# Seven block products in place of eight in the FFN up projections, with the down projection as a phase of its own

## The chip, the core and the metric

The kernel runs on one core of one Trainium2 chip. The metric is the device time of one execution in microseconds (us). Its engines, as the profile names them: PE (TensorE, matrix multiply), PEld (its weight loads, which run beside PE), DVE (VectorE), ACT (ScalarE), POOL (GpSimd), and SP, which only issues DMAs here. Each engine takes its instructions strictly in the order in which they were written into its queue, and waits on semaphores.

## What is computed

A decoder trunk of two layers on x of 1024 tokens by 1024 channels, in float32. Layer 0 has an attention mixer, layer 1 a gated recurrent one (RG-LRU); each is followed by a gated FFN with a short causal convolution, and a last norm ends the trunk. The change touches the two FFNs and what hands x to them:

```python
def conv_ffn(h, w_up, conv_w, conv_b, w_down):        # h 1024x1024, w_up 1024 x 5632
    u = causal_dwconv(h @ w_up, conv_w, conv_b)       # 3 taps along the tokens
    return (jax.nn.silu(u[..., :D_FF]) * u[..., D_FF:]) @ w_down   # D_FF 2816

x = x + mix                                           # for each layer
x = x + conv_ffn(rmsnorm(x, norm_ffn[layer]), f_w_up[layer], ...)
```

## The kernel before

Channels lie on the 128 partitions and tokens along a row, so x is 8 channel chunks (KC) by two token halves of 512 (HT). Every matmul multiplies a 128x128 weight block by a 128x512 operand in fp32r. To keep the precision, an operand is split into a rounded `hi` (ACT, L107 or L123) and the rest `lo` (DVE, L108 or L124), and `mm3` (L116) issues three matmuls: hi by hi, hi by lo, lo by hi (L118 to L120).

The FFN (`ffn`, L275) works through 22 chunks of 128 of the 2816 hidden channels. A chunk needs two up units, its gate half and its value half. `units` (L135) makes one unit with 2 halves x 8 KC x 3 = 48 matmuls into one of four PSUM tiles `U`. Its operand `H` (tiles hh and hl) is x times the norm's gain, made chunk by chunk in `norm_add` (L166) as each piece of x gets its last addend; the norm's factor per token, `R`, is multiplied in after the matmuls, when DVE takes the unit out of PSUM (L291). `rstd` (L198) makes R meanwhile from sums of squares: ACT squares each piece (L183), POOL adds the squares up (L187), PE sums over the partitions with a matrix of ones (L202), ACT takes Ln and Exp (L195, L196). After R comes the convolution (`conv`, L214: one ACT pass, then two DVE passes, L219 and L221), silu (ACT, L294), the product (DVE, L295) and the split into yh and yl, which stay in SBUF.

The down projection runs between the up units: after each group of four chunks (`UP_GROUPS`, L46) `down` (L231) multiplies the group's y by its weights, again with `mm3`, and DVE adds the result to x in SBUF (L227). The last group goes through `down_last` (L246), which hands each finished piece of x to the next norm. Weights come by SP from DRAM, 512 KB a transfer (L95), into two raw buffers `wr`, and are split into wh and wl.

The order on each engine is not the order of the code: a scheduler of the programming layer, which weighs priorities and free buffers, lays the instructions of all engines into their queues when the program is built. Every wait for a buffer that it hands out is part of that order.

Of the kernel before, what the change touches and what calls it, by code (L numbers as in the profile page):

```python
# [48 lines left out]
def half_of(h):  # L49
    return slice(h * HT, h * HT + HT)  # L50


class Kern:
# [62 lines left out]
    def mm3(self, out, whi, wlo, xhi, xlo, first, last):  # L116
        mm = self.nc.tensor.matmul
        mm(out, whi, xhi, start=first, stop=False)  # L118
        mm(out, whi, xlo, start=False, stop=False)  # L119
        mm(out, wlo, xhi, start=False, stop=last)  # L120
# [110 lines left out]
    def down(self, wsrc, ng, ys, bias=None):  # L231
        nf = 8 // ng
        for ft in range(8 // nf):
            w = self.load_w(wsrc(ft))
            for fi in range(nf):
                f = ft * nf + fi
                U = self.newU("D")
                for half in range(2):
                    sl = half_of(half)
                    for k in range(ng):  # L240
                        ws = slice((fi * ng + k) * P, (fi * ng + k + 1) * P)
                        self.mm3(U[:, sl], w[0][:, ws], w[1][:, ws], ys[k][0][:, sl], ys[k][1][:, sl], k == 0, k == ng - 1)
                for half in range(2):
                    self.accum(f, half, U[:, half_of(half)], bias)

    def down_last(self, wsrc, ng, ys, fin):  # L246
# [3 lines left out]
        for sl in fin.slices:  # L250
# [4 lines left out]
            for f0 in range(0, 8, 2):  # L255
                U = self.newU("D")
                for i in range(2):
                    f = f0 + i
                    w = ws_[f // nf]
                    for k in range(ng):  # L260
                        s = slice(((f % nf) * ng + k) * P, ((f % nf) * ng + k + 1) * P)
                        self.mm3(U[:, i * HT:i * HT + n], w[0][:, s], w[1][:, s], ys[k][0][:, sl], ys[k][1][:, sl], k == 0, k == ng - 1)
# [11 lines left out]

    def ffn(self, l, nm, fin):  # L275
        nc, io = self.nc, self.io
        fw, fb = f"fw{l}", f"fb{l}"
        with ExitStack() as st:
            hp = st.enter_context(self.pool(f"ffh{l}"))
            tp = st.enter_context(self.pool(f"fft{l}"))  # L280
            srcs = [io["wup"][l, ci, k] for ci in range(NFF) for k in range(2)]
            gen = self.units(srcs, nm["H"], 3, lambda: self.rstd(nm))
            ups = {}
            tmp = lambda: tp.tile([P, S], FP, tag="c", bufs=5, name=self.nm("c"))

            def up(ci):
                t = []
                for k in range(2):
                    U = next(gen)
                    z, o = tmp(), tmp()  # L290
                    nc.vector.tensor_tensor(z, U, nm["R"], op=OP.mult)  # L291
                    self.conv(o, z, (fw, fb), k * NFF + ci, 3)
                    t.append(o)
                nc.scalar.activation(t[0], t[0], AF.Silu)  # L294
                nc.vector.tensor_tensor(t[0], t[0], t[1], op=OP.mult)  # L295
                hi = hp.tile([P, S], FR, tag="y", bufs=10, name=self.nm("yh"))
                lo = hp.tile([P, S], FR, tag="y", bufs=10, name=self.nm("yl"))
                ups[ci] = self.split(hi, lo, t[0])

            def dn(g):  # L300
                c0, n = UP_GROUPS[g]
                ys = [ups.pop(c0 + i) for i in range(n)]
                if g == len(UP_GROUPS) - 1:
                    self.down_last(lambda ft: io["wdl"][l, ft], n, ys, fin)
                else:
                    self.down(lambda ft: io["wd"][l, g, ft], n, ys)

            for g, (c0, n) in enumerate(UP_GROUPS):
                last = g == len(UP_GROUPS) - 1
                for i in range(n):  # L310
                    up(c0 + i)
                    if i == (n - 1 if last else 0) and g > 0:
                        dn(g - 1)
            dn(len(UP_GROUPS) - 1)
# [25 lines left out]
    def rglru(self, nm, fin):  # L340
        nc, io = self.nc, self.io
        with ExitStack() as st:
            hp = st.enter_context(self.pool("rgh"))
            tp = st.enter_context(self.pool("rgt"))
            self.W2 = st.enter_context(self.pool("rgw"))
# [73 lines left out]
            G(7), Y(7), O(2), O(3)  # L419
            self.W2 = None  # L420

# [456 lines left out]
    def even_layer(self, fin):  # L878
# [4 lines left out]
        self.yd = [dp.tile([P, S], FP, name=f"yd{k}") for k in range(KC)]  # L883

# [253 lines left out]

class FinalNorm:
# [56 lines left out]
def open_main(k):  # L1196
# [3 lines left out]
    xp = k.ctx.enter_context(k.pool("X"))  # L1200
    k.X = [[xp.tile([P, HT], FP, name=f"x{c}_{h}") for h in range(2)] for c in range(KC)]
    k.np = k.ctx.enter_context(k.pool("np"))
    k.Rp = k.ctx.enter_context(k.pool("Rp"))
    hp = k.ctx.enter_context(k.pool("H"))
    k.Hp = [hp, hp]
    k.hbufs = 32

# [4 lines left out]
def trunk(tc, io, stages):  # L1212
    with ExitStack() as ctx:
# [5 lines left out]
        def finisher(i):  # L1219
            return NextNorm(k, GI[seq[i + 1]]) if i + 1 < len(seq) else FinalNorm(k)  # L1220
# [7 lines left out]
        else:  # L1228
            open_main(k)
            nm = k.new_norm(GI[seq[0]])  # L1230
            for half in range(2):
                for c in range(KC):
                    nc.sync.dma_start(k.X[c][half], io["x"][c, :, half_of(half)])
                    k.norm_add(nm, c, half, k.X[c][half])
# [30 lines left out]
```

## Time and profile before

| what | value |
|---|---|
| median of 3 runs | 2441.83 us (2440.38 to 2443.75) |
| the profiled execution | 2435.48 us, of which the span from first to last instruction is 2433.6 us |
| granted TensorE clock, mean over the span | 0.987 of full |
| attention layer's mixer | 0 to about 655 us |
| FFN of layer 0 | about 655 to 1388 us |
| recurrent mixer of layer 1 | about 1388 to 1690 us |
| FFN of layer 1, last norm, output | about 1690 to 2434 us |

A row of a group is read as: line, engine, operation, out<-in by the program's names, shapes, xcount, then the time in which the group was busy, the mean of one instruction, the engine's idle time before them and what ended it. In a timeline, a bracket behind a row gives the idle time of the engine before it and what it waited for. A matmul's own duration (about 0.39 us) covers its way through the array, and the next one starts before it ends, so the pace is the distance of two starts.

### The profile page before, as it was taken

What the parts mean: (1) busy time and instruction counts of PE and PEld (TensorE: products, weight loads), DVE (VectorE), ACT (ScalarE), POOL (GpSimd) and SP (SyncE); (2) the same over time, 40 slices, a digit from 0 to 9 for tenths busy, and PEclk for the clock granted to TensorE, in tenths of its full rate; (3) what the DMA queues carried; (4) which work ended last, traced back from release to release, by engine and by line L of the source; (5) the groups of instructions that cost most, each with busy time, mean ns of one, the idle gap of its engine ahead of it and who ended that gap; (6) DMA issues with size and microseconds to landing.
All of it is one profiled execution on the core that took longest, in us unless ns stands there. A gap on an engine that the chain in (4) does not pass through costs nothing.

```text
span 2433.6 us, 26552 instructions
## 1 busy us (share of the span) xinstructions
PE 2347.1 (96%) x10690; PEld 1925.2 (79%) x10690; DVE 1468.8 (60%) x2008; ACT 993.8 (41%) x1391; POOL 213.1 (9%) x151
## 2 busy tenths in 40 slices
PE   7899899999999999999999999999999999999997
PEld 5788777777688888888888777887888888888886
DVE  6456878988855453545455766768554535354556
ACT  5652767766632131213132465584322213131224
POOL 3002223211300000000000300003000000000001
PEclk9899999999999999999999999999999999999998
DMA  4113112222411111111111111111111111111111
GB/s 141 57 54 117 53 53 79 87 78 86 152 45 52 44 52 44 52 53 44 52 44 52 46 39 65 48 38 35 52 44 52 48 48 52 44 52 46 50 52 70
DMA packets 49435, 144.35 MB, mean 59 GB/s; under 512 B 5536, under 2 KB 9120, under 8 KB 49184
## 3 DMA queue, kind: packets, MB, share of 16 engines
q1 hardware_dynamic: 47808, 139.25, 16.7%
q8 instruction: 83, 1.36, 0.2%
q0 software_dynamic: 640, 2.10, 0.2%
q10 hardware_dynamic: 864, 1.32, 0.2%
q14 instruction: 40, 0.33, 0.0%
HBM read 130.06 MB, written 12.58 MB: 59 GB/s over the span
## 4 chain that ended last, share of the span: by engine, by line
PE 74%; DVE 8%; ACT 3%; issue 3%; POOL 1%; DMA 0%; DVEq 0%; SPq 0%; POOLq 0%; ACTq 0%
PE U L120 15%; PE U L119 15%; PE U L118 15%; PE D L118 7%; PE D L119 7%; PE D L120 7%; DVE hl L172 2%; PE T L764 2%; PE O L747 2%; PE F L118 1%; PE F L119 1%; PE F L120 1%; DVE P L739 1%; DVE x L266 1%; DVE P L722 1%
## 5 line engine op out<-in xcount | busy, mean ns | idle before, releaser
L118 PE MATMUL U<-hh,wh 128*128 128x512 f32 x1888 | 741.8, 393 | 16.6 <-ACT wh L107 15.0
L120 PE MATMUL U<-hh,wl 128*128 128x512 f32 x1888 | 741.8, 393 | 7.2 <-DVE wl L108 7.2
L119 PE MATMUL U<-hl,wh 128*128 128x512 f32 x1888 | 740.9, 393 | 7.6 <-DVE hl L172 7.6
L107 ACT ACTIVATE wh<-wr 128x1024 fp32r<-128x1024 f32 x208 | 220.5, 1060 | 833.4 <-PE U L119 469.5
L118 PEld LDWEIGHTS U<-hh,wh 128*128 128x128 f32 x1888 | 357.2, 189 | 94.6 <-ACT wh L107 16.6
L120 PEld LDWEIGHTS U<-hh,wl 128*128 128x128 f32 x1888 | 356.9, 189 | 87.5 <-DVE wl L108 12.2
L119 PEld LDWEIGHTS U<-hl,wh 128*128 128x128 f32 x1888 | 357.4, 189 | 85.6 <-DVE hl L172 10.3
L291 DVE TENSOR_TENSOR c<-U,R 128x1024 f32<-128x1024 f32 x88 | 107.8, 1225 | 388.5 <-PE U L120 371.4
L118 PE MATMUL D<-yh,wh 128*128 128x512 f32 (+1 forms) x720 | 278.0, 386 | 0.0
L119 PE MATMUL D<-yl,wh 128*128 128x512 f32 (+1 forms) x720 | 277.2, 385 | 0.0
L120 PE MATMUL D<-yh,wl 128*128 128x512 f32 (+1 forms) x720 | 277.2, 385 | 0.0
L227 DVE TENSOR_TENSOR x<-D,x 128x512 f32<-128x512 f32 x192 | 123.6, 685 | 236.7 <-PE D L120 236.6
L108 DVE TENSOR_TENSOR wl<-wr,wh 128x1024 fp32r<-128x1024 f32 x184 | 231.7, 1260 | 48.6 <-ACT wh L107 45.4
L221 DVE SCALAR_TENSOR_TENSOR c<-c,par,c 128x1023 f32<-128x1023 f32 (+1 forms) x176 | 225.7, 1283 | 17.9 <-ACT c L219 15.0
L187 POOL TENSOR_TENSOR sq<-sq,sq 128x512 f32<-128x512 f32 x56 | 89.1, 1597 | 1036.4 <-ACT sq L183 995.7
L118 PEld LDWEIGHTS D<-yh,wh 128*128 128x128 f32 x720 | 135.8, 189 | 27.2 <-DVE x L266 0.2
L119 PEld LDWEIGHTS D<-yl,wh 128*128 128x128 f32 x720 | 135.8, 189 | 27.1 <-issue 0.2
L120 PEld LDWEIGHTS D<-yh,wl 128*128 128x128 f32 x720 | 135.8, 189 | 26.7
L219 ACT ACTIVATE c<-c,par 128x1024 f32<-128x1024 f32 x88 | 109.6, 1245 | 37.4 <-DVE c L291 37.4
L123 ACT ACTIVATE yh<-c 128x1024 fp32r<-128x1024 f32 x44 | 46.7, 1060 | 175.4 <-DVE c L295 159.8
L724 ACT ACTIVATE P<-P,m 128x640 f32<-128x640 f32 (+7 forms) x128 | 93.5, 730 | 46.4 <-DVE m L722 46.0
L124 DVE TENSOR_TENSOR pl<-T,ph 128x512 fp32r<-128x512 f32 x132 | 89.3, 686 | 28.7 <-ACT ph L123 26.1
(258 smaller groups left out, 2938.4 us busy)
## 6 DMA issues: line engine op xcount, KB each, us to landing
wr<-in_wup SPq DMA_DIRECT2D x88, 512.0 KB, 3.2
wr<-in_wd SPq DMA_DIRECT2D x40, 512.0 KB, 3.2
wr<-in_wbc SPq DMA_DIRECT2D x24, 512.0 KB, 3.4
wr<-in_cin SPq DMA_DIRECT2D x16, 512.0 KB, 3.2
yd<-y SPq DMA_DIRECT2D x24, 256.0 KB, 2.3
x<-in_x SPq DMA_DIRECT2D x16, 256.0 KB, 5.8
wr<-in_wob SPq DMA_DIRECT2D x8, 512.0 KB, 3.3
y<-in_x SPq DMA_DIRECT2D x16, 256.0 KB, 2.6
```

The costliest lines, as they stand in the source:

```text
L107: nc.scalar.activation(hi[:, s], raw[:, s], AF.Copy)
L108: eng.tensor_tensor(lo[:, s], raw[:, s], hi[:, s].bitcast(FP), op=OP.subtract)
L118: mm(out, whi, xhi, start=first, stop=False)
L119: mm(out, whi, xlo, start=False, stop=False)
L120: mm(out, wlo, xhi, start=False, stop=last)
L124: (eng or self.nc.vector).tensor_tensor(lo, t, hi.bitcast(FP), op=OP.subtract)
L187: eng.tensor_tensor(acc, acc, t, op=OP.add)
L219: nc.scalar.activation(o, src, AF.Identity, bias=b, scale=w(K - 1))
L221: nc.vector.scalar_tensor_tensor(o[:, s:], src[:, :n - s], w(K - 1 - s), o[:, s:], op0=OP.mult, op1=OP.add)
L227: nc.vector.tensor_tensor(x, ps, x, op=OP.add)
L291: nc.vector.tensor_tensor(z, U, nm["R"], op=OP.mult)
L724: nc.scalar.activation(p, p, AF.Exp, bias=m, scale=-1.0, accum_out=s)
```

## The change

Of a hidden chunk, the gate and value halves of the weights (128 channels each) by the two halves of the input channels (512 each) make a 2x2 block matrix a11, a12, a21, a22; the normed x, by the two halves of the input channels and the two halves of the tokens, makes b11, b12, b21, b22. The plain product takes eight block products. The changed `ffn` takes seven (`up_units`), each of 4 KC x 3 = 12 matmuls of 128x512, from sums of blocks.

- Sums of weight blocks, per chunk: four POOL adds of 128x512 (`up_sums`, into tiles z: s1 and s2 in one, s3 and s4 in the other), then splits of z on ACT and DVE (tiles sh and sl; ah and al for a22). Two buffers of each.
- Sums of x blocks, once per layer: 16 POOL adds (`ProductNorm.finish`), and splits into "pages": 56 tiles hi and lo for the seven operands.
- R and the gain are now multiplied into x before it is split (`ProductNorm.half`, 16 DVE operations of 128x512 per layer), so the operand exists only once R does. The operation after PSUM (L291 before) goes.
- The seven products accumulate in three PSUM banks A, Bk, C of a chunk. `begin(i + 1)` (products "1" and "2") is written ahead of `rest(i)` (products "6", "5", "7", "3", "4"); ACT copies of 128x512 (L337, L348, L350, L356 in the new numbering) and three DVE adds take the four results out.
- x itself is stored to DRAM (xd) before the FFN and loaded back after the up phase, and its SBUF serves the up phase. The gated values go to DRAM through POOL's queue (fd), 512 KB each, and come back for the down phase, which runs after all 22 chunks; their split into hi and lo moves there.
- The recurrent mixer closes its temporary pools before its last `down`.

The core of the diff:

```diff
+    def up_sums(self, raws):
+        p = self.nc.gpsimd
+        a11, a12, a21, a22 = (raws[k][:, half_of(h)] for k in range(2) for h in range(2))
...
+        p.tensor_tensor(s1, a21, a22, op=OP.add)
+        p.tensor_tensor(s2, s1, a11, op=OP.subtract)
+        p.tensor_tensor(s3, a11, a21, op=OP.subtract)
+        p.tensor_tensor(s4, a12, s2, op=OP.subtract)
...
+        w12 = self.split(t(S, "sh", 2), t(S, "sl", 2), sa)
+        w34 = self.split(t(S, "sh", 2), t(S, "sl", 2), sb)
+        wa = self.split(t(HT, "ah", 2), t(HT, "al", 2), a22)
...
+        def begin(i):
+            raws[i] = self.up_raw(srcs[i])
+            w = self.split_w(raws[i][0])
...
+            self.product(A, at(0), B["1"], True)
+            nc.scalar.activation(z[0][:, :HT], A, AF.Copy)
+            self.product(C, at(1), B["2"], True)
+            nc.vector.tensor_tensor(z[0][:, :HT], C, z[0][:, :HT], op=OP.add)
...
+        def rest(i):
...
+            self.product(A, w["6"], B["6"], False)
+            nc.scalar.activation(c12, A, AF.Copy)
+            self.product(Bk, w["5"], B["5"], True)
+            nc.scalar.activation(c22, Bk, AF.Copy)
+            self.product(A, w["7"], B["7"], False)
+            v(c22, A, c22, op=OP.add)
+            self.product(Bk, w["3"], B["3"], False)
+            v(c12, Bk, c12, op=OP.add)
+            self.product(A, w["4"], B["4"], False)
+            nc.scalar.activation(c21, A, AF.Copy)
...
+    def add(self, f, half, x):
+        k = self.k
+        k.nc.sync.dma_start(k.xd[f][:, half_of(half)], x)
+        k.sq_add(self.st, half, x, k.nc.gpsimd)
...
+            nc.vector.scalar_tensor_tensor(X[c], X[c], k.pv("g", self.st["gi"] * KC + c), R, op0=OP.mult, op1=OP.mult)
+            if h == 0:
+                p = "12"[c // 4]
+                self.B[p][c % 4] = k.pages(p, X[c])
...
+    def finish(self):
+        self.half(1)
...
+        for i in range(4):
+            b11, b12, b21, b22 = b[i][0]
+            op(b11, b12, b11, op=OP.subtract)
+            B["3"][i] = k.pages("3", b22)
+            op(b12, b22, b12, op=OP.subtract)
+            op(b22, b22, b11, op=OP.subtract)
+            B["6"][i] = k.pages("6", b22)
+            op(b21, b21, b22, op=OP.subtract)
```

What the scheduler makes of it at three places. **First, ACT where layer 0's FFN begins.** Before, the squares (sq, L183) stand between the hi splits of x (hh, L171) and of the mixer's last weights (wh, L107):

```order
L123 ACTIVATE og1111_5886<-ofb2_3356 128x512
L183 ACTIVATE sq1128_6030<-x0_0_5952 128x512
L123 ACTIVATE og1113_5890<-ofb3_3357 128x512
L183 ACTIVATE sq1134_6042<-x1_0_5954 128x512
L107 ACTIVATE wh1123_5995<-wr1122_5993 128x1024
L171 ACTIVATE hh1126_6026<-x0_0_5952,par_58 128x512
L107 ACTIVATE wh1139_6054<-wr1138_6052 128x1024
L171 ACTIVATE hh1129_6032<-x0_1_5953,par_58 128x512
L183 ACTIVATE sq1131_6036<-x0_1_5953 128x512
```

Now all 16 squares (L190) stand behind the third of these weight splits:

```order
L130 ACTIVATE og1113_5920<-ofb3_3387 128x512
L114 ACTIVATE wh1139_6025<-wr1138_6023 128x1024
L114 ACTIVATE wh1147_6072<-wr1146_6070 128x1024
L114 ACTIVATE wh1155_6121<-wr1154_6119 128x1024
L190 ACTIVATE sq1142_6057<-x0_01122_5991 128x512
L190 ACTIVATE sq1143_6060<-x0_11123_5992 128x512
L190 ACTIVATE sq1144_6063<-x1_01124_5993 128x512
```

The x splits hh are gone from here, and no square is taken until that third split is done.

**Second, POOL at the same place.** Before, its last weight split of the mixer is followed by the adds of squares, 14 of them, and then by nothing until the next norm:

```order
L108 TENSOR_TENSOR wl1066_5684<-wr1064_5681,wh1065_5683 128x1024
L187 TENSOR_TENSOR sq1128_6030<-sq1128_6030,sq1134_6042 128x512
L187 TENSOR_TENSOR sq1131_6036<-sq1131_6036,sq1137_6049 128x512
L187 TENSOR_TENSOR sq1128_6030<-sq1128_6030,sq1144_6089 128x512
L187 TENSOR_TENSOR sq1131_6036<-sq1131_6036,sq1147_6096 128x512
```

Now, behind the 14 adds, come the four sums of chunk 0's weights (z, L302 to L305), the 16 sums of x blocks in turn (L1292 to L1297; four of their lines are shown), the sums of the next two chunks, and then the first store of gated values:

```order
L194 TENSOR_TENSOR sq1143_6060<-sq1143_6060,sq1166_6208 128x512
L302 TENSOR_TENSOR z1241_6456<-wr1227_6383 128x512
L304 TENSOR_TENSOR z1242_6457<-wr1226_6381,wr1227_6383 128x512
L303 TENSOR_TENSOR z1241_6456<-z1241_6456,wr1226_6381 128x512
L305 TENSOR_TENSOR z1242_6457<-wr1226_6381,z1241_6456 128x512
L1292 TENSOR_TENSOR x0_01122_5991<-x0_11123_5992,x0_01122_5991 128x512
L1294 TENSOR_TENSOR x0_11123_5992<-x4_11131_6000,x0_11123_5992 128x512
L1292 TENSOR_TENSOR x1_01124_5993<-x1_11125_5994,x1_01124_5993 128x512
L1294 TENSOR_TENSOR x1_11125_5994<-x5_11133_6002,x1_11125_5994 128x512
```

POOL has 20 more operations between the norm and the first products of `rest(0)`.

**Third, ACT in the up phase.** Before, a unit's weight split stands beside the convolution's pass (c) and the split of y; nothing that PE waits for at once stands behind it:

```order
L107 ACTIVATE wh1220_6562<-wr1219_6560 128x1024
L219 ACTIVATE c1210_6488<-c1209_6487,par_58 128x1024
L123 ACTIVATE yh1211_6495<-c1204_6427 128x1024
L107 ACTIVATE wh1228_6629<-wr1227_6627 128x1024
L219 ACTIVATE c1218_6555<-c1217_6554,par_58 128x1024
L294 ACTIVATE c1218_6555<-c1218_6555 128x1024
L107 ACTIVATE wh1234_6690<-wr1233_6688 128x1024
```

Now the copies out of PSUM stand in the same queue (AB holds the banks A and Bk of a chunk):

```order
L337 ACTIVATE z1344_7217<-AB1343_7216 128x512
L114 ACTIVATE wh1376_7475<-wr1374_7471 128x1024
L348 ACTIVATE z1327_7086<-AB1325_7084 128x512
L130 ACTIVATE sh1366_7383<-z1364_7377 128x1024
L350 ACTIVATE z1328_7087<-AB1325_7084 128x512
L130 ACTIVATE sh1368_7387<-z1365_7378 128x1024
L226 ACTIVATE c1354_7328<-z1327_7086,par_58 128x1024
L130 ACTIVATE ah1387_7522<-wr1357_7341 128x512
L356 ACTIVATE z1328_7087<-AB1325_7084 128x512
L226 ACTIVATE c1355_7332<-z1328_7087,par_58 128x1024
L381 ACTIVATE c1354_7328<-c1354_7328 128x1024
L337 ACTIVATE z1362_7349<-AB1360_7347 128x512
```

The copy of product "6" (L348) stands here behind the weight split wh of the chunk two further on (L114). In the next chunk L348 stands ahead of it. Of the 44 chunks of both layers, 16 have the order shown, in every second chunk from the seventh on.

## Rows read from the trace of the kernel before

**Rows 1.** The page, section 1: busy time, share of the span, instructions.

```profile
span 2433.6 us, 26552 instructions
PE 2347.1 (96%) x10690; PEld 1925.2 (79%) x10690; DVE 1468.8 (60%) x2008; ACT 993.8 (41%) x1391; POOL 213.1 (9%) x151
```

**Rows 2.** Busy time by stretch: us, each engine's busy time (instructions), clock, DMA.

```profile
700.00:1360.00 660.00, 660.00 (x2914) 546.67 (x2913) 329.68 (x308) 161.82 (x146) 0.00 (x0) 1.00 0.14 49
1730.00:2400.00 670.00, 670.00 (x2961) 554.89 (x2960) 337.21 (x321) 168.66 (x157) 0.00 (x0) 1.00 0.14 48
655.00:700.00 45.00, 40.68 (x163) 31.56 (x162) 25.89 (x21) 19.31 (x24) 12.70 (x7) 0.92 0.14 47
1684.00:1720.00 36.00, 31.39 (x127) 24.16 (x126) 14.98 (x14) 12.91 (x17) 7.83 (x6) 0.95 0.08 30
```

**Rows 3.** Timeline of PE where layer 0's FFN begins: start, us, instruction.

```profile
655.43 0.40 PE L120 MATMUL W<-og,wl 128*128 128x512 f32 x1
655.66 0.39 PE L118 MATMUL U<-hh,wh 128*128 128x512 f32 x1
657.72 0.50 PE L120 MATMUL U<-hh,wl 128*128 128x512 f32 x1 [1.44 <-DVE wl L108]
661.08 0.80 PE L118 MATMUL U<-hh,wh 128*128 128x512 f32 x1 [2.40 <-ACT wh L107]
661.68 0.63 PE L119 MATMUL U<-hl,wh 128*128 128x512 f32 x1
662.10 0.63 PE L120 MATMUL U<-hh,wl 128*128 128x512 f32 x1
```

**Rows 4.** Timeline of ACT at that place: a weight split, then R.

```profile
644.43 1.06 ACT L107 ACTIVATE wh<-wr 128x1024 fp32r<-128x1024 f32 x1 [0.58 <-ACT hh L171]
688.09 1.12 ACT L195 ACTIVATE R<-ss,eps 128x1024 f32<-128x1024 f32 x1 [6.27 <-PE ss L202]
```

**Rows 5.** Timeline of POOL where layer 1 begins.

```profile
1369.66 3.16 POOL L187 TENSOR_TENSOR sq<-sq,sq 128x512 f32<-128x512 f32 x2 [0.86 <-ACT sq L183]
1373.69 1.30 POOL L187 TENSOR_TENSOR sq<-sq,sq 128x512 f32<-128x512 f32 x1 [0.87 <-ACT sq L183]
1379.27 1.30 POOL L187 TENSOR_TENSOR sq<-sq,sq 128x512 f32<-128x512 f32 x1 [0.41 <-ACT sq L183]
1383.45 5.15 POOL L187 TENSOR_TENSOR sq<-sq,sq 128x512 f32<-128x512 f32 x3 [2.88 <-ACT sq L183]
```

**Rows 6.** Timeline of DVE in the same stretch.

```profile
1368.75 1.22 DVE L108 TENSOR_TENSOR wl<-wr,wh 128x1024 fp32r<-128x1024 f32 x1
1369.88 1.78 DVE L172 SCALAR_TENSOR_TENSOR hl<-x,par,hh 128x512 fp32r<-128x512 f32 x1
1379.33 0.68 DVE L266 TENSOR_TENSOR x<-D,x 128x512 f32<-128x512 f32 x1
1381.64 0.73 DVE L172 SCALAR_TENSOR_TENSOR hl<-x,par,hh 128x512 fp32r<-128x512 f32 x1
1382.30 1.28 DVE L266 TENSOR_TENSOR x<-D,x 128x512 f32<-128x512 f32 x2
1385.19 2.28 DVE L108 TENSOR_TENSOR wl<-wr,wh 128x1024 fp32r<-128x1024 f32 x1
```

**Rows 7.** Groups by line: busy us, mean ns | idle before, releaser.

```profile
L107 ACT ACTIVATE wh<-wr 128x1024 fp32r<-128x1024 f32 x208 | 220.5, 1060 | 833.4 <-PE U L119 469.5
L221 DVE SCALAR_TENSOR_TENSOR c<-c,par,c 128x1023 f32<-128x1023 f32 (+1 forms) x176 | 225.7, 1283 | 17.9 <-ACT c L219 15.0
L123 ACT ACTIVATE ph<-T 128x512 fp32r<-128x512 f32 x132 | 76.3, 590 | 41.5 <-PE T L764 25.3 <-PE O L747 15.4
```

**Rows 8.** DMA issues: xcount, KB each, median us to landing; POOL's time for one.

```profile
wr<-in_wup SPq DMA_DIRECT2D x88, 512.0 KB, 3.2
ob<-bo POOLq DMA_DIRECT2D x8, 256.0 KB, 2.7
L512 POOL DMA_DIRECT2D ob<-bo x8: 582/588/712, 194.0 to 396.0; - x8
```

More of the change, by code (lines that the diff above doesn't have):

```diff
@@ L50, in half_of, with cols @@
     return slice(h * HT, h * HT + HT)
+def cols(y, sl):
+    if not isinstance(y, list):
+        return y[:, sl]
+    z = sl.start // HT
+    return y[z][:, sl.start - z * HT:sl.stop - z * HT]
 class Kern:
@@ L273, in down_last, with pages, page, up_raw @@
         fin.done(prev)
+    def pages(self, p, xn):
+        hi, lo = (self.page(p) for _ in range(2))
+        return self.split(hi, lo, xn)
+    def page(self, p):
+        pool, bufs = (self.Bp, 24) if p in "374" else (self.Ap, 32)
+        return pool.tile([P, HT], FR, tag="h", bufs=bufs, name=self.nm("h"))
+    def up_raw(self, src):
+        raws = [self.load_raw(src[0])]
+        raws.append(self.W3.tile([P, S], FP, tag="wr", bufs=2, name=self.nm("wr")))
+        self.nc.sync.dma_start(raws[1], src[1])
+        return raws
@@ new lines, in ffn, with ys @@
+        self.main_open()
+        for half in range(2):
+            for f in range(KC):
+                nc.sync.dma_start(self.X[f][half], self.xd[f][:, half_of(half)])
+        with self.pool(f"yr{l}", side="right") as yr, self.pool(f"y{l}", side="right") as yp:
+            def ys(g):
+                c0, n = UP_GROUPS[g]
+                out = []
+                for ci in range(c0, c0 + n):
+                    raw = yr.tile([P, S], FP, tag="yr", bufs=2, name=self.nm("yr"))
+                    nc.sync.dma_start(raw, self.fd[ci])
+                    if g < 2:
+                        hl = [self.pages("1", raw[:, half_of(h)]) for h in range(2)]
+                        out.append([[hl[h][k] for h in range(2)] for k in range(2)])
+                    else:
+                        t = lambda: yp.tile([P, S], FR, tag="y", bufs=10, name=self.nm("y"))
+                        out.append(self.split(t(), t(), raw))
+                return out
+            cur = ys(0)
+            for g, (c0, n) in enumerate(UP_GROUPS):
@@ L303, in dn @@
                 if g == len(UP_GROUPS) - 1:
-                    self.down_last(lambda ft: io["wdl"][l, ft], n, ys, fin)
+                    self.down_last(lambda ft: io["wdl"][l, ft], n, cur, fin)
                 else:
[L306 to L313, printed above, removed]
@@ L314, in ffn, with main_open @@
-            dn(len(UP_GROUPS) - 1)
+                    nxt = ys(g + 1)
+                    self.down(lambda ft: io["wd"][l, g, ft], n, cur)
+                    cur = nxt
+    def main_open(self):
+        self.mst = [ExitStack() for _ in range(3)]
+        en = lambda i, name: self.mst[i].enter_context(self.pool(name))
+        self.np, self.Rp, xp = en(2, "np"), en(1, "Rp"), en(0, "X")
+        self.X = [[xp.tile([P, HT], FP, name=self.nm(f"x{c}_{h}")) for h in range(2)] for c in range(KC)]
@@ L1228, in trunk @@
         else:
[L1229 to L1234, printed above, removed]
+            raise ValueError("the first stage is attention")
         for i in range(i0, len(seq)):
```

137 lines of the change are left out of this document (99 added, 38 removed).

## The prediction, made before the changed kernel was run

> **What bounds the kernel now.** I read the page's busy times first, then busy time by stretch, then the timelines where a stage begins. PE is busy for 96% of the span [rows 1]; the reader is to see next that this is no average over slack. In the stretches 700 to 1360 us and 1730 to 2400 us, most of both FFNs, PE never waits: 660.00 us for 2914 matmuls, which is 0.2265 us each, while DVE is busy for half of the stretch and POOL not at all [rows 2]. So a matmul that is left out there is worth its 0.2265 us, as long as nothing that takes its place makes PE wait. At the beginning of the FFN the trace shows how the present kernel avoids a gap: the last matmul of the mixer starts at 655.43 and the first up matmul at 655.66, since x goes in before its norm factor is known [rows 3]. Then come waits of 1.44 and 2.40 us, and after them matmuls 0.43 us apart instead of 0.23: the granted clock of that stretch is 0.92, so for a part of it the lower of two levels, 1.2 instead of 2.4 GHz [rows 2, 3]. In 45 us PE started 163 matmuls, worth 36.9, so this entrance costs 8.1 us; layer 1's costs 36 less 127 x 0.2265, 7.2 us [rows 2].
>
> **What the change removes.** The up phases shrink from 2 x 22 x 96 to 2 x 22 x 84 matmuls: 528 x 0.2265 = 119.6 us, all on the bound engine. The DVE pass after PSUM and the R behind it go too; they lay beside PE and are worth nothing.
>
> **The entrance, layer 0.** Now no up matmul can start before R. By the order on ACT, no square is taken until the mixer's third weight split is done, which in the trace ended at 644.43 + 1.06 = 645.5 [rows 4]. Three squares later, at about 647, POOL begins its 14 adds; one that runs alone takes 1.30 [rows 5], so they end at 665.3. The sum over partitions, Ln and Exp of the halves take about 2.7 (Ln of both halves took 1.12 [rows 4]): R at 668, 12.2 us behind the last matmul's end at 655.8.
>
> From there to the first product of rest(0), DVE has 16 multiplications by gain and R and 28 lo splits of pages, 44 operations of 128x512, and four lo splits of 128x1024. POOL has 18 of its 20 adds left. The question is whether the two run side by side. Alone, a DVE operation on two SBUF tiles of 512 columns takes 0.73 and lets the next start after 0.66; 1024 columns take 1.22, pitch 1.13. Beside a POOL add, the same operations took 1.78 and 2.28 [rows 6], and two POOL adds 3.16 instead of 2.60, three 5.15 instead of 3.90 [rows 5]. They take turns. A DVE operation that reads PSUM does not: 0.68 while POOL's add of 1379.27 ran [rows 5, 6]. So times add up: 44 x 0.66 + 4 x 1.13 + 18 x 1.30 = 29.0 + 4.5 + 23.4 = 57 us. PE has only 60 matmuls of products "1" and "2" meanwhile, 13.6 us. It loses 12.2 + 57 - 13.6 = 55.6, less the 8.1 of before: +47.5.
>
> **The entrance, layer 1.** Here the first token half is normed while the last down still multiplies the second half (48 matmuls, 10.9 us), which hides R of that half and 16 of the DVE operations (10.6). R of the other half comes about 5 us after the last matmul (add to x 0.68, square 0.6, POOL's add 1.30, then sum, Ln and Exp). 5 + 46.4 - 13.6 = 37.8, less 7.2: +30.6.
>
> Both entrances: +78. If DVE and POOL overlapped fully, DVE's 33.5 and 22.9 alone would be left, +24 and +7, so +31; the upper bound is 98, with another 10 us each of queue waits. I take 78, as the rows show turns. Matmuls after such waits ran 0.43 apart [rows 3]; for the some 20 next to the resumption I add 4 us an entrance, **+8**.
>
> **The loop of the up phase.** Per chunk PE needs 84 x 0.2265 = 19.0. DVE's work is four splits (3 x 1.22 + 0.7), four taps of 1.28, the product 1.2 and three PSUM adds of 0.68: 12.7; with POOL's four adds (5.2) in turns at most 17.9. ACT has about 10. No engine is over PE, but the queues are in order and there are two buffers of each, which makes a ring. Product "3" of a chunk ends; this frees sh, and ACT splits the next z (1.06 [rows 7]); DVE makes its lo (1.22); this frees z, and POOL adds s3 and s4 for the chunk after, in turns with DVE's taps (1.28 each [rows 7]), 2 x 1.30 + 2 x 1.0 = 4.6; this frees the raw weights, and SP loads the next (3.2 [rows 8]); ACT splits them (1.06). In 16 of 44 chunks the copy of product "6" stands behind that split on ACT (0.59 [rows 7]), and product "5" on PE waits for the copy. From there to the end of product "3" are 47 matmuls, 10.65. Sum: 1.06 + 1.22 + 4.6 + 3.2 + 1.06 + 0.59 + 10.65 = 22.4, which is 3.4 over PE's 19.0: 16 x 3.4 = **+54**. In the other 28 the copy stands ahead, but that of product "5" stays behind the split; its waiter on PE comes some 12 matmuls later, so I take 0.5 each, **+14** (0 to 2 each). A wait of 3.4 is of the size of the two in [rows 3], after which 12 matmuls lost 0.2 each; for half of 16 such waits that is **+19** (0 to 40). No row shows taps beside POOL, since POOL idles in that stretch [rows 2]: if they did not take turns the ring would be 20.4, and the 54 would be 22. The nearest rows, two-input operations of the same size, say turns, so I keep 54; if DVE's other work were in the way too, another 2 us in each round would make it 86.
>
> The Trainium skill (SBUF — State Buffer, section Who interferes with whom) says that a DVE instruction with two SBUF inputs and a GpSimd instruction that reads SBUF exclude each other for the whole instruction. By that rule the taps do take turns, and the sum stays as it is; by the rows alone it could be 32 us lower. The skill's GPSIMD Engine Reference (Engine selection) says that elementwise work belongs on VectorE, GpSimd being about twice as slow. Rows 5 and 6 agree (1.30 against a pitch of 0.66), and this speaks against the placement: with the sums on DVE the entrances would be about 23 us shorter.
>
> **What lies beside.** Stores of x and loads back, 4 MB each per layer, go by SP in the entrance and at the change of phase; the loads back are needed one by one, 5.4 us apart, as down finishes each chunk, and four PSUM tiles give slack. Gated values: POOL spends 0.59 on a store [rows 8], after DVE's product is there, and POOL's next sums stand behind it; that is inside the ring's slack of the other chunks, and costs up to 0.6 a chunk if not. Down has the same 1056 matmuls per layer and its splits on idle engines. For the change of phase I take 3 us a layer, **+6** (0 to 10).
>
> **Sum.** -119.6 + 78 + 8 + 54 + 14 + 19 + 6 = +59. The profiled execution took 2435.5 (span 2433.6 and 1.9 around it), 6.3 below the median of the runs; on the median the forecast is 2441.8 + 59 = 2501, said as 2500.
>
> **Rivals.**
> - *DVE and POOL overlap where I make them take turns.* Entrances +31, ring +22: -119.6 + 31 + 4 + 22 + 14 + 5 + 6 = -38, 2404. Against it stand 1.78 and 2.28 beside 0.73 and 1.22 [rows 6]; for it, that only two kinds of operation are seen there. 7%.
> - *The ring has slack that I don't see* (the copy seldom late), the entrances as forecast: -119.6 + 78 + 8 + 6 = -28, 2414. It decides if the ring is under 19.0, so if 3.4 us fall out of 22.4. 6%.
> - *The ring closes in every chunk from the seventh on*, 32 of them, because the copy of product "5" is as late as that of "6": another 16 x 3.4 - 8 + 19 = +65, 2566. For it: both copies stand behind a split that waits for a load of 3.2. 12%.
> - *The change does what it says and all else hides behind PE*: only the wait for R stays, -119.6 + 12 + 5 + 6 = -97, 2345. The port rows speak against it. 2%.
>
> **How the numbers follow.** Forecast 73%. The range goes from 2455, where about half of the turns are hidden, to 2560, the third rival's lower edge; outside it lie the faster rivals (15%) and a part of the third. A measurement of this kernel can tell about 0.2% (5 us) from no change. Faster: the first, second and fourth rival less what of them ends near nothing, 13%; within: 4%; slower: 83%.
>
> **What would show it.** In the changed profile: some 528 PE instructions fewer; about 55 and 40 us from each mixer's last matmul to the first product of rest(0) in which PE is idle, with DVE and POOL busy in turn and DVE's 512-column operations near 1.8; in the up phase two chunks in 41 to 44 us instead of 38, with PE's waits released by ACT's copy (L348) and ACT waiting before it for a load; down without gaps. Wrong would be an entrance under 25 us, or chunks at 19.0 throughout.

## The result, and the profile after

The changed kernel takes 2556.63 us (median, 2554.99 to 2558.01) against 2441.69 us: a ratio of 1.047, 95% interval [1.0452, 1.0488], so 115 us slower where +59 was forecast. The profiled execution has a span of 2554.6 us, 121.0 more than before [rows 1]. Its page, section 1 (busy time, share of the span, instructions), is to be set beside [rows 1]:

```profile
span 2554.6 us, 26846 instructions
PE 2328.7 (91%) x10162; PEld 1841.7 (72%) x10162; DVE 1658.0 (65%) x2212; ACT 1154.9 (45%) x1699; POOL 595.7 (23%) x403
```

PE has 528 instructions fewer, as computed, worth 119.6 us at 0.2265. Yet its busy time fell by 18 us only: a busy matmul takes longer here than before. The stretches show it, this time cut at the stage boundaries (length; busy time and instructions of PE, PEld, DVE, ACT, POOL; granted clock; DMA). In order: layer 0's entrance (from the mixer's last matmul to the first product "6"), its up phase, its change of phase and down; then the same for layer 1:

```profile
663.31:731.22 67.91, 25.28 (x67) 15.68 (x65) 52.80 (x52) 30.76 (x50) 46.02 (x31) 0.65 0.19 70
731.22:1207.43 476.21, 445.39 (x1803) 341.61 (x1802) 308.05 (x264) 196.56 (x241) 157.63 (x104) 0.97 0.21 76
1207.43:1454.78 247.35, 242.99 (x1043) 196.63 (x1041) 123.00 (x180) 59.38 (x72) 13.69 (x10) 0.99 0.29 98
1752.70:1811.61 58.91, 22.35 (x64) 14.27 (x63) 54.58 (x53) 27.04 (x44) 35.24 (x23) 0.68 0.07 24
1811.61:2286.04 474.43, 442.30 (x1804) 339.47 (x1802) 306.56 (x264) 196.40 (x241) 158.19 (x104) 0.97 0.21 77
2286.04:2525.50 239.46, 236.06 (x1031) 192.11 (x1029) 111.67 (x145) 53.69 (x63) 0.53 (x1) 0.99 0.28 97
```

Each length less its matmuls at 0.2265 is what that stretch loses. An up phase has 1802 matmuls, 408.2 us, and took 476.2 and 474.4: 68.1 and 66.3 lost, or 134.4. I split these by the distance of two matmul starts: idle time that PE's records show before a matmul (30.8 + 32.1 = 62.9), together with the 8.3 by which the matmul ahead of each such wait runs out alone, in about 0.39 in place of 0.2265; 116 distances of some 0.43, all at the lower granted clock (24.4 over 0.2265); 207 single distances of about 0.33, most of them between the first and the second matmul of a product (22.1); and the rest, a pace of 0.230 to 0.234 in place of 0.2265 (16.6).

| term | forecast | measured |
|---|---|---|
| 528 matmuls left out | -119.6 | -119.6 |
| entrance of layer 0 (with its slow matmuls) | +51.5 | +46.2 |
| entrance of layer 1 (with its slow matmuls) | +34.6 | +38.1 |
| up phases: waits of PE, with the matmul that runs out before each | +68 | +71.2 |
| up phases: slow clock | +19 | +24.4 |
| up phases: distances of 0.33 | 0 | +22.1 |
| up phases: pace | 0 | +16.6 |
| change of phase and down | +6 | +18.0 |
| the two mixers | 0 | +7.9 - 2.5 |
| sum | +59.5 | +122.4 (span: +121.0) |

Who waits for whom on PE (total us, times, longest): the copies of the products "6" (L348) and "5" (L350), which the forecast named, are the first row and a later one.

```profile
PE AB L125 <- ACT z L348: 49.4, 20, 3.8
PE AB L127 <- DVE wl L115: 28.3, 4, 15.4
PE ss L1271 <- POOL sq L194: 16.9, 2, 8.9
PE C L125 <- DVE z L339: 16.6, 1, 16.6
...
PE AB L125 <- ACT z L350: 11.3, 25, 2.0
```

**The ring, in one round.** Timelines of four engines in layer 1 (start, us, engine, line, operation, [idle before and what ended it]). ACT splits z, DVE makes the lo, POOL makes s3 and s4, the freed raw buffer is loaded, ACT splits the load, and only then takes the copy for which PE waits:

```profile
2019.16 1.06 ACT L130 ACTIVATE sh<-z 128x1024 fp32r<-128x1024 f32 x1 [6.91 <-PE AB L126]
2020.26 1.23 DVE L131 TENSOR_TENSOR sl<-z,sh 128x1024 fp32r<-128x1024 f32 x1 [0.22 <-ACT sh L130]
2021.41 3.51 DVE L228 SCALAR_TENSOR_TENSOR c<-z,par,c 128x1023 f32<-128x1023 f32 x2
2021.56 2.28 POOL L304 TENSOR_TENSOR z<-wr,wr 128x512 f32<-128x512 f32 x1 [5.53 <-DVE sl L131]
2023.80 2.27 POOL L305 TENSOR_TENSOR z<-wr,z 128x512 f32<-128x512 f32 x1
2030.63 1.06 ACT L114 ACTIVATE wh<-wr 128x1024 fp32r<-128x1024 f32 x1 [3.84 <-DMA wr<-in_wup]
2031.59 0.58 ACT L348 ACTIVATE z<-AB 128x512 f32<-128x512 f32 x1
2032.22 0.80 PE L125 MATMUL AB<-h,sh 128*128 128x512 f32 x1 [3.81 <-ACT z L348]
2032.82 0.63 PE L126 MATMUL AB<-h,sh 128*128 128x512 f32 x1
2033.24 0.63 PE L127 MATMUL AB<-h,sl 128*128 128x512 f32 x1
2045.41 1.06 ACT L130 ACTIVATE sh<-z 128x1024 fp32r<-128x1024 f32 x1 [6.91 <-PE AB L126]
```

From split to split it is 26.25 us: 1.1 + 1.3 + 4.6 for POOL's two turns, as forecast, then 4.6 for the load in place of 3.2 (the page gives these loads a median of 4.2 us to landing, before 3.2 [rows 8]), 1.0 and 0.6 on ACT, and 13.2 in place of 10.65 from the copy to the end of product "3", since the matmuls behind the wait are 0.42 apart at first. The round before it, in which the copy stands ahead of the split, took 19.9 (ACT's split at 1999.26). Two chunks take 46.2 us; 41 to 44 were forecast. The rows also answer what no row of before could: DVE's taps do take turns with POOL's adds. Two taps took 3.51 us here and 2.59 right after the adds (from 2026.55); the adds beside them took 2.28 and 2.27, where one without them took 1.29 (from 2013.38). The mean tap is 1.49 in this kernel; with the adds on DVE (e4_wsums_dve below) it is 1.28 again.

**The entrance.** POOL's squares end later than I put them (673.8 instead of 665.3), but the mixer ended 7.9 us later too; from the last matmul to DVE's first multiplication by R it is 14.4 us. Then DVE and POOL take turns: two-input operations of DVE at 1.75 beside POOL's, 0.74 before, and POOL's x sums at 1.6 to 2.3, 1.27 alone.

```profile
656.48 17.33 POOL L194 TENSOR_TENSOR sq<-sq,sq 128x512 f32<-128x512 f32 x14 [41.92 <-ACT sq L190]
677.69 2.99 DVE L1279 SCALAR_TENSOR_TENSOR x<-x,par,R 128x512 f32<-128x512 f32 x3 [12.66 <-ACT R L203]
685.67 0.74 DVE L1279 SCALAR_TENSOR_TENSOR x<-x,par,R 128x512 f32<-128x512 f32 x1
687.80 2.26 POOL L1292 TENSOR_TENSOR x<-x,x 128x512 f32<-128x512 f32 x1 [8.99 <-DVE x L1279]
688.86 1.75 DVE L1279 SCALAR_TENSOR_TENSOR x<-x,par,R 128x512 f32<-128x512 f32 x1
690.14 1.59 POOL L1294 TENSOR_TENSOR x<-x,x 128x512 f32<-128x512 f32 x1
```

### The profile page after: what moved, and what is told of

It is laid out like the page before. It is cut to its first block, busy times and chain, and to the rows that moved or that the text cites. A ratio compares the mean times of both kernels' runs of the same rounds, so it can differ in the third digit from the quotient of the medians.

```text
span 2554.6 us, 26846 instructions
## 1 busy us (share of the span) xinstructions
PE 2328.7 (91%) x10162; PEld 1841.7 (72%) x10162; DVE 1658.0 (65%) x2212; ACT 1154.9 (45%) x1699; POOL 595.7 (23%) x403
## 5 line engine op out<-in xcount | busy, mean ns | idle before, releaser
L114 ACT ACTIVATE wh<-wr 128x1024 fp32r<-128x1024 f32 x164 | 173.5, 1058 | 513.2 <-PE D L126 281.8
L125 PE MATMUL AB<-h,sh 128*128 128x512 f32 x704 | 300.0, 426 | 62.7 <-ACT z L348 49.4
L126 PE MATMUL AB<-h,sh 128*128 128x512 f32 x704 | 285.3, 405 | 0.0
L127 PE MATMUL AB<-h,sl 128*128 128x512 f32 x704 | 284.6, 405 | 0.0
L228 DVE SCALAR_TENSOR_TENSOR c<-z,par,c 128x1023 f32<-128x1023 f32 (+1 forms) x176 | 262.2, 1490 | 7.6 <-ACT c L226 4.4
L125 PEld LDWEIGHTS AB<-h,sh 128*128 128x128 f32 x704 | 136.8, 194 | 134.7 <-ACT z L348 64.0
L125 PE MATMUL U<-hh,wh 128*128 128x512 f32 x480 | 192.4, 401 | 11.4 <-ACT wh L114 11.4
L126 PE MATMUL U<-hl,wh 128*128 128x512 f32 x480 | 191.8, 401 | 7.8 <-DVE hl L179 7.8
L127 PE MATMUL U<-hh,wl 128*128 128x512 f32 x480 | 191.7, 400 | 1.7 <-DVE wl L115 1.7
L125 PE MATMUL D<-y,wh 128*128 128x512 f32 (+1 forms) x464 | 181.0, 392 | 0.0
L126 PE MATMUL D<-y,wh 128*128 128x512 f32 (+1 forms) x464 | 180.8, 390 | 0.0
L127 PE MATMUL D<-y,wl 128*128 128x512 f32 (+1 forms) x464 | 180.8, 390 | 0.0
L127 PEld LDWEIGHTS AB<-h,sl 128*128 128x128 f32 x704 | 137.8, 196 | 32.7
L126 PEld LDWEIGHTS AB<-h,sh 128*128 128x128 f32 x704 | 138.3, 196 | 26.6
L302 POOL TENSOR_TENSOR z<-wr 128x512 f32<-128x512 f32 x44 | 58.3, 1325 | 417.8 <-PE D L127 251.0
```

What stands on the lines that cost most here:

```text
L114: nc.scalar.activation(hi[:, s], raw[:, s], AF.Copy)
L125: mm(out, whi, xhi, start=first, stop=False, skip_group_check=resumed)
L126: mm(out, whi, xlo, start=False, stop=False, skip_group_check=resumed)
L127: mm(out, wlo, xhi, start=False, stop=last, skip_group_check=resumed)
L228: nc.vector.scalar_tensor_tensor(o[:, s:], src[:, :n - s], w(K - 1 - s), o[:, s:], op0=OP.mult, op1=OP.add)
L302: p.tensor_tensor(s1, a21, a22, op=OP.add)
```

## The experiments

Ten variants were run, each beside the kernel before; its median was 2442.8, 2443.0 and 2444.1 us in the three groups (e1 to e4, e5 to e8, e9 and e10). Two questions were open: what makes the loop lose 134 us (the ring, or something beside it), and what the two terms are that no step of the prediction has, the pace and the distances of 0.33.

### e1_align: operand tiles moved by 32 bytes

The down phase of the changed kernel changes its pace when it passes from tiles `h` to tiles `y`: 222 matmuls in 50 us and then 598 in 140 (first fence below). A window also counts a matmul that only reaches into it, for up to 0.39 us, so these are 50.4 by 222, 0.227, and 140.4 by 598, 0.235. The slow tiles began at an odd multiple of 32 bytes.

```diff
             self.W3 = right.enter_context(self.pool(f"W3{l}", side="right"))
+            self.W3.tile([P, 8], FP, name=self.nm("pad"))
...
+            yr.tile([P, 8], FP, name=self.nm("pad"))
```

> Only a pad of 32 bytes in two pools, so that the operand tiles that began at an odd multiple of 32 bytes (pages of products 3, 7 and 4, and y of the down phase) begin at a multiple of 64; order and waits stay. In the changed kernel's trace matmuls on such tiles started 0.234 us apart and those on tiles at a multiple of 64 0.227. Theory A, the start address sets the pace: 2 x (22 x 36 + 14 x 48) = 2928 matmuls gain 0.0075 us each, 22 us, so about 2535, and the pace of the down phase is 0.2265 throughout. Rival, the pace there comes from something else of those stretches: no change, 2556, and 0.234 stays.

2556.3 us (2548.4 to 2559.4), ratio 1.0469 [1.0452, 1.0487]: no change. Stretches of the down phase on `h` and on `y` in the changed kernel, and on `y` here:

```profile
1240.00:1290.00 50.00, 50.00 (x222) 41.42 (x221) 21.93 (x28) 8.39 (x8) 0.00 (x0) 1.00 0.28 95
1310.00:1450.00 140.00, 140.00 (x598) 112.23 (x597) 66.28 (x84) 31.95 (x38) 10.01 (x7) 1.00 0.22 72
```

```profile
1310.00:1440.00 130.00, 130.00 (x558) 104.13 (x557) 60.55 (x77) 29.44 (x34) 6.95 (x5) 1.00 0.23 73
```

130.4 by 558 is 0.234: theory A falls in this form. A multiple of 64 bytes isn't it.

### e2_banks: one PSUM tile for each accumulator

A chunk's accumulators A and Bk are two banks of one tile AB, and the program's waits are kept by tile. In the trace a product waits for the take-out of the one just before it, though that lies in the other bank.

```diff
-            ab = self.newU("AB")
-            if i % 2 == 0:
-                cp[0] = self.newU("C")
-            A, Bk, C = ab[:, :HT], ab[:, HT:], cp[0][:, half_of(i % 2)]
+            A, Bk, C = self.bank("A", 3), self.bank("Bk", 3), self.bank("C", 2)
```

(`bank` gives a tile [P, HT] of its own in a PSUM pool that is opened for the up phase; the lines that open and close the pool are left out here.)

> The two accumulators of a chunk (A and Bk) become two PSUM tiles of one bank each, three of each, and C a tile of its own, in place of one tile AB of two banks; nothing else. Waits are kept by tile, so a product that goes into one bank then no longer waits for the copy or add that empties the other. Theory A, the loop's loss (about 134 us in both layers: 63 us of waits, the rest a lower clock behind them and some 0.1 us at the beginning of each product) hangs on these waits: the waits fall under 15 us, and the time falls by 70 to 100 us, to 2460 to 2490. Rival, the ring of buffers (split, POOL's sums, load) is longer than a chunk by itself: the copies come late all the same, and less than 25 us are gained.

2425.1 us (2421.5 to 2428.1), ratio 0.9927 [0.9909, 0.9946]: 131 us less than the changed kernel, more than either theory said, and faster than the kernel before. 116 of it lie in the up phases (134.4 lost there before, 18.4 here, 13 of it pace), the rest at the entrances and the changes of phase. PE no longer waits in the up phase (2.3 us in all), and chunks follow every 19.3 us. The stretch 800 to 1100 in layer 0's up phase, first of the changed kernel, then of this one:

```profile
800.00:1100.00 300.00, 279.24 (x1119) 214.61 (x1118) 189.27 (x160) 119.13 (x146) 102.93 (x68) 0.95 0.19 71
```

```profile
800.00:1100.00 300.00, 300.00 (x1307) 245.16 (x1306) 225.61 (x188) 143.90 (x171) 110.43 (x78) 1.00 0.23 82
```

The ring's links are all still there. On ACT the copy of product "6" (L352 in this kernel's numbering) still follows the split that waits for its load:

```profile
2014.91 1.06 ACT L114 ACTIVATE wh<-wr 128x1024 fp32r<-128x1024 f32 x1 [0.98 <-DMA wr<-in_wup]
2016.06 0.60 ACT L352 ACTIVATE z<-A 128x512 f32<-128x512 f32 x1
```

But product "5" goes into its own tile and no longer waits for that copy; the next that does is "7", 2.7 us later. The distances of 0.33 are gone too (207 before, 4 here), so they hung on the shared tile as well: short waits of the same kind. And with the waits went the lower clock: 1.00 in the stretch, 0.95 before. The edit also lets A and Bk have three buffers each, where AB and C shared four tiles; more tiles of two banks alone were not tried. They would not part product "5" from the copy of "6", since both lie in the one tile of a chunk.

### e3_xsums_dve: the sums of x blocks on DVE

```diff
-        op = k.nc.gpsimd.tensor_tensor
+        op = k.nc.vector.tensor_tensor
```

> Only the 16 sums of x blocks per layer move from POOL to DVE. Theory A, DVE and POOL take turns at the entrance, so the times add: 16 x 0.66 = 10.6 us stand there in place of 16 x 1.3 to 1.7 = 21 to 27, and each entrance is 10 to 16 us shorter, so 2525 to 2537. Rival, they overlap and DVE alone sets the entrance: 10.6 us longer each, 2578.

2551.6 us (2549.1 to 2553.8), ratio 1.0446 [1.043, 1.0461]: 5 us less. Neither theory has this. DVE's part went as theory A says: every operation is back at 0.68 to 0.74, and from its first multiplication to its last page split it took 39 us (673.9 to 713.1) in place of 49 (677.7 to 726.5). PE got little of it. Its timeline:

```profile
712.53 0.80 PE L127 MATMUL AB<-h,wl 128*128 128x512 f32 x1 [27.67 <-DVE wl L115]
```

The lo split of chunk 0's weights now stands on DVE behind all the x sums. In the changed kernel 36 of the first products' 60 matmuls had run by 713.6, beside DVE's work. Here 6 of 48 had run when the split came, and the other 42 run behind DVE's work, the first 12 or so 0.43 apart, at the lower clock (granted clock 0.77 from 712.53 to 724.89). From DVE's first multiplication to the first product "6" it is 51.0 us instead of 53.5.

### e4_wsums_dve: the sums of weight blocks on DVE

```diff
-        p = self.nc.gpsimd
+        p = self.nc.vector
```

> Only the four weight sums per chunk move from POOL to DVE. Theory A, POOL's adds, in turns with DVE, are the long part of the ring (POOL's four took about 1.3 to 2.2 us each, on DVE 0.66): the ring shortens by 3 us or more, and with it most of the waits of 1 to 4 us go, 40 to 80 us, 2475 to 2515. Rival, the ring closes elsewhere (load of 4.2 us, ACT's order, PSUM waits): under 15 us are gained, or, as DVE comes to about 15.5 us of 19 per chunk, its queue turns late and time is lost.

2470.4 us (2470.0 to 2473.1), ratio 1.0116 [1.0101, 1.0131]: 86 us less, a little over theory A. A chunk takes 19.9, and 8 us of waits are left in the up phases. So POOL's turns were a link of the ring as well: with 0.68 in place of 2.3 for each of s3 and s4 the loads come in time. The Trainium skill (GPSIMD Engine Reference, section Engine selection) puts elementwise work on VectorE; for these sums the run bears it out. What stays of the loss (22.5 and 24.4 us an up phase) is mostly the 0.33 at the start of products (over 180 of them) and the pace.

### e5_places: operand tiles at four places

```diff
-            self.W3.tile([P, 8], FP, name=self.nm("pad"))
+            self.W3.tile([P, (168, 248)[l]], FP, name=self.nm("pad"))
...
-            yr.tile([P, 8], FP, name=self.nm("pad"))
+            yr.tile([P, (168, 504)[l]], FP, name=self.nm("pad"))
```

(against e1_align; the accumulators as in e2_banks.)

> The kernel of e2_banks, with pads ahead of the page and y tiles so that they begin elsewhere; order and waits as in e2_banks. In e1_align a move by 32 bytes left the slow pace (0.2333 for 0.2343). Every fast operand tile of the traces begins 1344 bytes past a multiple of 2048, as do all the weight tiles; the slow ones began at 2016 (e1_align: 1984). Theory A, the place within 2048 bytes sets the pace: layer 0's pages of products 3, 7, 4 and its y, now at 1344, start 0.2265 apart; layer 1's pages at 1024 and its y at 0 differ from that and from each other. The gain over e2_banks (2425) is then some 11 us from layer 0 and 0 to 11 from layer 1: 2403 to 2415. Rival, the pace belongs to the region or the phase: 0.233 to 0.234 in all four, and 2425.

2417.4 us (2415.4 to 2421.6), ratio 0.9897 [0.9881, 0.9913], 7.7 less than e2_banks, where theory A named 10 or more; the ranges of the two touch. Between the profiled executions it is 12.3, of which 7.1 lie in the up phases and about 5 in layer 0's matmuls on y. Matched with the program's addresses, distances at full clock had these means: pages at 1344 bytes past a multiple of 2048 0.227 (layer 0), at 1024 0.233 (layer 1), at 2016 0.234 (e2_banks, both layers); y at 1344 0.227, at 0 0.233, at 2016 0.234 (e2_banks, both layers). The down phases on y, layer 0 and layer 1:

```profile
1250.00:1370.00 120.00, 119.94 (x528) 98.61 (x527) 58.47 (x74) 28.58 (x34) 7.25 (x5) 1.00 0.24 79
2250.00:2350.00 100.00, 100.00 (x430) 80.08 (x429) 42.82 (x53) 17.85 (x17) 0.00 (x0) 1.00 0.25 82
```

120.4 by 528 is 0.228 (0.06 idle in it), 100.4 by 430 is 0.2335. So the place where the operand's tile begins does set the pace, and region and phase don't. A distance from the weights within 2048 bytes isn't it: weight blocks begin at 320, 832, 1344 and 1856 past a multiple of 2048, and operands at 1344 kept 0.227 beside each of the four. All four lie 320 past a multiple of 512, as 1344 does, so a distance from the weights within 512 bytes, or a period shorter than 2048, stays open.

### e6_z3: a third buffer for z

```diff
-        sa, sb = (self.W3.tile([P, S], FP, tag="z", bufs=2, name=self.nm("z")) for _ in range(2))
+        sa, sb = (self.W3.tile([P, S], FP, tag="z", bufs=3, name=self.nm("z")) for _ in range(2))
```

> The changed kernel with a third buffer for the tiles z of the weight sums, nothing else: POOL's sums for the next chunk no longer wait for DVE's lo split to free z. Theory A, the ring of the prediction (split of z, lo, sums of the next chunk, load, split, copy, products) sets the chunk's time: its link through z is open, so most of the 63 us of waits and some of the slow clock go, 50 to 100 us, 2455 to 2505. Rival, what holds the chunks is the bank waits (a product waits for the take-out of the one just before it) with ACT's order: under 20 us are gained, 2537 to 2557.

2528.9 us (2527.5 to 2532.8), ratio 1.0354 [1.0338, 1.0369]: 28 us less, between the theories. The loads now come in time, and ACT's split no longer waits for one. But the scheduler put another waiting operation ahead of the copy, the silu of the chunk before, which waits for DVE's taps:

```profile
2032.57 1.06 ACT L381 ACTIVATE c<-c 128x1024 f32<-128x1024 f32 x1 [1.96 <-DVE c L228]
2033.53 0.58 ACT L348 ACTIVATE z<-AB 128x512 f32<-128x512 f32 x1
```

```profile
PE AB L125 <- ACT z L348: 38.0, 21, 2.7
```

As many waits for this copy as before (21, and 20 in the changed kernel), each shorter. The ring decided how late the copy is; that PE stands at once when the copy is late is the shared tile's doing.

### e7_best_a and e8_best_b: the gains together

e2_banks with the pages and y of both layers at 1344, x sums on DVE, and the sums of squares on DVE; e8_best_b has the weight sums there too. (The first pair of lines is against e5_places, the second against the changed kernel; the pad of y and the lines of the other runs are left out.)

```diff
-            self.W3.tile([P, (168, 248)[l]], FP, name=self.nm("pad"))
+            self.W3.tile([P, 168], FP, name=self.nm("pad"))
...
-        k.sq_add(self.st, half, x, k.nc.gpsimd)
+        k.sq_add(self.st, half, x, k.nc.vector)
```

> e2_banks, and the pages and y at 1344 bytes past a multiple of 2048, the x sums on DVE, and the sums of squares ahead of the FFNs on DVE in place of POOL. From e2_banks (2425): x sums 5 to 9 (e3_xsums_dve), sums of squares 17.3 us on POOL to about 10 on DVE, which stands idle then, so R some 7 us earlier in layer 0 and 0 to 3 in layer 1; pace 0 or 22 by the theories of e5_places. 2385 to 2412. A rival: the entrance is bound by DVE from R on and by loads, so the squares bring nothing: 2395 to 2420.

> e7_best_a with the weight sums on DVE too, so that POOL does no sums at all. In the loop of e2_banks no wait is left, so the loop gains nothing there; the entrance loses POOL's first sums (4 adds that ran before R at no cost now stand on DVE) and gains the turns. DVE is busy about 15.5 of 19.3 us of a chunk. Theory A, same within 5 us of e7_best_a. Rival, DVE's longer queue delays an add or a lo split that PE waits for: 10 to 40 us slower than e7_best_a (e4_wsums_dve kept 19.9 a chunk in place of 19.3).

2397.7 us (2396.3 to 2399.1), ratio 0.9815 [0.9799, 0.9831], and 2388.4 (2386.4 to 2396.2), 0.9782 [0.9762, 0.9802]. In the up phase both run at the pace of the kernel before: in e8_best_b 1325 matmuls in 300 us, chunks every 19.0. DVE at 77% of that stretch is no bound:

```profile
800.00:1100.00 300.00, 300.00 (x1325) 248.40 (x1324) 230.66 (x253) 144.35 (x172) 8.52 (x16) 1.00 0.24 85
```

e8_best_b came out 9 us under e7_best_a, where 5 were named; the medians' ranges nearly meet. What is left lies in the entrances, and there is the wait of e3_xsums_dve again:

```profile
714.77 0.80 PE L127 MATMUL A<-h,wl 128*128 128x512 f32 x1 [27.47 <-DVE wl L115]
```

### e9_early and e10_early_pool: the first weights ahead of R

```diff
+            pre = [self.up_w(io["wup"][l, ci]) for ci in range(2)]
             nm.finish()
...
-            raws[i] = self.up_raw(srcs[i])
-            w = self.split_w(raws[i][0])
+            raws[i], w = pre[i] if i < len(pre) else self.up_w(srcs[i])
```

(`up_w` does the two lines taken out; e10_early_pool leaves the weight sums on POOL.)

> e8_best_b, with the loads and splits of the first two chunks' weights (wh, wl) written ahead of R and the x sums. In e8_best_b product 1 of chunk 0 waited 27.5 us in layer 0 and 16.9 us in layer 1 for its lo split wl, which stood on DVE behind the x sums, so the 48 matmuls of products 1 and 2 of the first two chunks ran after DVE's work instead of beside it. Theory A: they now run beside it, 10.9 us and some 3 us of slow clock less in each entrance, 20 to 28 us, 2360 to 2370. Rival: the pages of products 1 and 2 are as late as wl, or DVE's later work sets the first product 6 alone, so the matmuls move but the first product 6 doesn't: less than 8 us, 2380 to 2390.

> e9_early with the weight sums back on POOL. Theory A: in a loop without bank waits it is equal which engine sums, and at the entrance POOL's first eight adds can run before R or beside: within 6 us of e9_early. Rival: turns with DVE at the entrance (8 adds of 1.3 to 2.2 us) and in the loop cost 8 to 15 us more.

2386.5 us (2382.2 to 2387.7), ratio 0.9772 [0.9752, 0.9791], and 2394.4 (2386.2 to 2396.7), 0.9811 [0.9788, 0.9833]. Theory A of e9_early falls: 2 us less than e8_best_b, inside the rival's range. In layer 0 the wait for wl is gone and the entrance loses 39.6 us instead of 47.9; PE now waits there for the split of the weight sums (first row). In layer 1 the lo split still stands behind the x sums on DVE (second row):

```profile
710.04 0.80 PE L125 MATMUL A<-h,sh 128*128 128x512 f32 x1 [21.47 <-ACT sh L130]
...
1706.75 0.80 PE L127 MATMUL A<-h,wl 128*128 128x512 f32 x1 [16.45 <-DVE wl L115]
```

The medians show less of layer 0's 8 us than the profiled executions, which lie 14 us apart: that of e8_best_b is the slowest of its four, that of e9_early the fastest. e10_early_pool is 8 us behind e9_early with overlapping ranges, so the two are not told apart. e9_early has the lowest median of all, 2.3% under the kernel before, but its range overlaps that of e8_best_b.

## Why the prediction was right, and where it was short

The measured time lies in the range, 3 us below its upper end, and the sign is right. That it lies inside is in part luck: the sum has no term for the short waits at the starts of products (22.1) and none for the pace (16.6 in the up phases, about 10 in down), and nothing else of that size came on top. The number comes close to the third rival (2566), but its mechanism isn't what happened: the copy of product "5" was late 25 times by 0.45 on average (11.3 us), as the forecast's +14 has it, and not by 3.4.

- **Matmuls left out**: right, 528.
- **Entrances**: right, 84 us against 86, with R 14.4 us behind the last matmul in place of 12.2 and 16 POOL adds beside DVE in place of 18. The turns that it rests on [rows 5, 6] are seen beside the x sums: DVE's 0.74 becomes 1.75, POOL's 1.27 becomes 1.6 to 2.3. The Trainium skill (SBUF — State Buffer, section Who interferes with whom) has them as an exclusion for the whole instruction; the trace agrees: twelve lo splits of pages from 711.31 took 11.64 us, some 7.3 alone, with three POOL adds and a part of a fourth beside them. The sum counted DVE's and POOL's operations and took PE's 13.6 us off as running beside; e3_xsums_dve shows that this last step holds only by the order on DVE.
- **The ring, waits**: right in place and size, 71.2 against 68 (62.9 idle, 8.3 of matmuls running out): the copy behind the split, every second chunk, 3.8 at the longest against 3.4. Two of its durations were low (the load, 4.6 against 3.2; the run to product "3", 13.2 against 10.65). But the ring was taken as the cause by itself. e2_banks and e4_wsums_dve each cut another link, and each takes nearly all of the waits away (2.3 and 8 us are left). The prediction named the link that is cheapest to cut, that product "5" on PE "waits for the copy", without asking why it should.
- **The step that was short**: the loop's sum. Beside the long waits it has only the clock behind them, "A wait of 3.4 is of the size of the two in [rows 3] ... for half of 16 such waits that is +19". The lower clock came to 24.4, near that. But the starts of products (22.1) have no term, since the sum counts a product's waits only where they are long; 207 short ones weigh as much as six long ones do. e2_banks removed them with the long ones, which shows that they hung on the shared tile, as waits for the other bank's take-out would.
- **Pace**: no term either, and no row of the stretches that I read would have given it, since every FFN operand of the kernel before lies at the good place. The rate "0.2265 us each" [rows 2] was carried over to tiles at other places. Up phases: 2 x 792 matmuls on pages at 2016 by 0.0074 are 11.7 of the 16.6; down: 2 x 672 by 0.0077 are 10.3 of the 18.0. In layer 0 of e5_places and in both layers of e8_best_b these went.
- **Change of phase**: PE waits 4.4 us in layer 0 and 3.4 in layer 1 for DVE's adds to x, 7.8 against 6. In layer 1 DVE waits there for x to come back; in layer 0 DVE is busy between the adds with small operations of the next mixer (ls, from 1225.6 to 1227.9), which the forecast didn't have. The rest is the pace above.
- **The mixers**: the attention mixer, whose work is untouched, ended 7.9 us later. The granted clock of the first 100 us was 0.96 before (first row) and 0.91 now (second row):

```profile
0.00:100.00 100.00, 74.45 (x335) 58.75 (x335) 60.88 (x70) 65.59 (x78) 24.29 (x20) 0.96 0.30 105
```

```profile
0.00:100.00 100.00, 77.36 (x325) 60.99 (x326) 58.87 (x64) 61.67 (x72) 24.64 (x20) 0.91 0.30 104
```

In the profiled variants its last matmul started between 657.1 and 666.8. I count it as scatter from build to build; why it falls to one side is open.

Between the spans the forecast is 61.5 us short (56 between the medians, since the profiled execution of before lay 6.3 under its median): 47.3 in the up phases (starts 22.1, pace 16.6, clock 5.4, waits 3.2), 12.0 at the change of phase and in down, 5.4 in the mixers, -1.8 at the entrances, and -1.4 that I can't assign. The first and second rival fell with the turns and the waits that the trace shows. Most rows named as tests held: 528 instructions fewer, 54 and 45 us lost at the entrances (55 and 40 named), PE's waits released by L348, ACT before it waiting for a load. Two did not: two chunks took 46.2 us, over the 41 to 44 named, and down has a gap at its start in each layer.

## What to carry to other kernels

A product that is left out pays only if PE's next operand and next accumulator are ready: cutting the wait between two banks of one tile turned 4.7% slower into 0.7% faster with the same operations on the same engines. Price a loop's short waits by their number as well as the long ones by their length, and look at which link of a ring is only bookkeeping before costing its engines. And a rate per matmul holds for the operands that it was read from: where tiles move in SBUF, look at the pace again.

## What the runs showed of the hardware

A matmul of 128x512 whose moving operand begins 1344 bytes past a multiple of 2048 followed the one before after 0.227 us, at 0, 1024, 1984 and 2016 bytes after 0.232 to 0.235, at full granted clock: 3%, with order, weights and waits alike (e2_banks against e5_places). The kernel before has it as well, in its attention mixer, where operands lie at 1984 and 2016 (means 0.232 to 0.234).
